# A decoder layer whose instruction order comes from a list scheduler: VectorE and GpSimd booked as taking turns, a new stage order, and a gated branch that keeps its keys as logarithms

## The chip, the core and the metric

The kernel runs on one core of a Trainium2 chip. A core has TensorE (PE, matrix products), VectorE (DVE), ScalarE (ACT), GpSimd (POOL), SyncE (SP, which starts the transfers here) and 16 DMA engines. The metric is the time of one execution on the device in microseconds. The kernel before took 1223.98 us, the median of three runs of 1223.35, 1223.98 and 1227.55 us.

## The reference, cut to what matters

One decoder layer with three token mixers side by side, for a prompt of 512 tokens and for 8 sequences of 8 new tokens (576 columns in all), everything in fp32. The model width is 1024; each mixer has 4 heads.

```python
proj = jnp.einsum('bld,dn->bln', h, w_in[l])      # aq af ai ag | bq bk bv bo bi bf | cx cg cb ca | mg
a_logf = jnp.log(lb + (1.0 - lb) * jax.nn.sigmoid(af32))
a_k = (1.0 - lb) * jax.nn.sigmoid(-af32)
# branch a (HGRN2), per chunk:
b = jnp.cumsum(fc, axis=2)
att = einsum('bhtk,bhsk,bhtsk->bhts', qc, kc, exp(b_t - b_s))     # t >= s
o = einsum('bhtk,bhkv->bhtv', qc * jnp.exp(b), S) + einsum('bhts,bhsv->bhtv', att, vc)
S_new = exp(bl) * S + einsum('bhsk,bhsv->bhkv', kc * jnp.exp(bl - b), vc)
# branch b (mLSTM): the same shape with a running maximum m and a normaliser n
# branch c (gated DeltaNet): short convolution, l2-normalised q and k, and per chunk
sol = triangular_solve(eye + a, rhs)              # a strictly lower triangular
# after the branches
z = einsum('blnc,ncd->blnd', ys, w_branch);  merged = sum(sigmoid(mg) * z)
h = layer_norm(ALPHA * h + merged @ w_out)        # LN1
gate, up = split(h @ w_ffn_in)
h = layer_norm(ALPHA * h + (silu(gate) * up) @ w_ffn_out)         # LN2
```

## The kernel before, in words

Columns of 128 features stand on the partitions and the 576 tokens (in two halves of 288) are the moving columns of a matrix product. Each fp32 product is made of three products of rounded halves, `xh*wh + xl*wh + xh*wl`. So each block of weights that lands by DMA (`wr`) is rounded by ScalarE into `wh`, and VectorE subtracts to get `wl`. A projection of 128 features, tile `p`, is 48 TensorE instructions (8 blocks of the inner dimension x 3 products x 2 halves). It can't finish before its `wl` is there.

The stages have two-letter names. `v00` to `v32` are the convolutions of branch c (first digit the head, second q, k or v), `rc` and `rb` the rows of scalar gates, `di` the inverse of the triangular matrices of branch c, `p0`-`p4` its preparations by chunk, `c1`-`c4` its chunk steps, `C0`-`C3` its sampled states. `h0`-`h3` are the heads of branch a, `a1`-`a4` and `A0`-`A3` its chunk steps and sampled states, `B1`-`B4` the chunk steps of branch b. `cA`, `aA`, `bA` load sampled states. `Z`, `X` and `Y` with a digit are the merge of the branches (gate projections, branch projections, sums), then come LN1, the feed-forward network (tiles `pq`, `us`, `fg`, `fl`, and `g` for its second product) and LN2.

Three places matter for what follows.

**The inverse in branch c** (`di`). On 64 partitions VectorE runs a recurrence over the diagonals: each step is a product `dp<-dX,dY` and a sum `dY<-dY,dp`, and each needs the one before. The rows of weights' `wl` stand in the same queue.

**The heads of branch a** (`a_head`, from L1132). Per head: the key `ak` from the gate, the cumulated log decay `ab`, and seven levels. A level computes `z`, the decay from a block's middle: a subtraction (sites `a` and `b`), one exponential, then a multiplication of one half by the key (`c`) and of the other half by the query (`d`, `z<-z,gate`), and TensorE multiplies the halves (`pz`). Twenty-eight levels in all. A last factor `akd` gives the keys decayed to the chunk's end.

**LN1.** The mean and the mean square of LN1 are first accumulated over the feature blocks (`acc<-acc,lr` and `acc<-acc,lsq`), then rounded (`ch`, `cl`), summed over the partitions by TensorE (`os`), and turned into `rstd` and `m`; then `lr<-lr,rstd`, `lr<-lr,m`, and the halves `hh`, `hl`, which the network's products read. The network's products are made by a Strassen-like scheme whose weight sums (`S`, `S3l`, `wL`, `wl`) are formed at the same time.

**What sets the order.** No instruction is issued where it is written. The `Plan` (from L61) records every operation with the tiles that it reads and writes; `schedule()` then runs the whole program on a model of the engines: it has a cost for each operation (`cost`), latencies between engines (`LAT`), free buffers, a model of TensorE's half-speed windows, and a slowdown while VectorE and GpSimd work at once (`PORT`). Always the instruction that can start first is taken, ties by priority. The priority is the place of a stage in the string `ORDER` (between `-` and `+` a stage goes one level earlier). `FLEX` lists sites whose operation may go to either of two engines; the model picks the one that would be done first. All instructions are then issued from one line, L434, so the profile's rows are told apart by tile. The chip's engines each run their own list in order and wait for one another by semaphores.

```python
for e, fn, a, k, cost, lock in o.alts:
    t = max(o.ready, eft[e]) + cost * (PSLOW if e == "POOL" else 1.0)
    ...
    if best is None or t < best:
        best = t
```

Of the kernel before, what the change touches and what calls it, by code (L numbers as in the profile page):

```python
# [11 lines left out]
ALU = mybir.AluOpType  # L12
# [51 lines left out]
class Plan:  # L64
# [35 lines left out]
    def cost(self, eng, name, out, a, k):  # L100
# [14 lines left out]
        if eng == "ACT":  # L115
            return 95 + 0.834 * n + 93 * cols
# [32 lines left out]
    def add(self, eng, name, fn, a, k):  # L149
# [47 lines left out]
    def table(self, name, after):  # L197
# [5 lines left out]
        o.cost, o.nb, o.tiles, o.alts, o.lock, o.act = 1300.0, 0, [], None, 0, 0.0  # L203
        self.ops.append(o)
# [49 lines left out]
    def schedule(self):  # L254
# [53 lines left out]
        busy = {"DVE": (0.0, 0), "POOL": (0.0, 0)}  # L308
# [30 lines left out]
        while len(order) < len(ops):  # L339
# [37 lines left out]
            if o.eng == "PE":  # L377
# [10 lines left out]
                if cold:  # L388
                    took += act
# [6 lines left out]
            elif o.eng in busy:  # L396
                dve = o.eng == "DVE"
                till, lock = busy["POOL" if dve else "DVE"]
                if o.lock and lock and till > s_:
                    v, g = (o.lock, lock) if dve else (lock, o.lock)  # L400
                    kv = PORT[v, g]
                    kg = 0.33 if v == 1 else 0.2
                    both = min(till - s_, took / (1 - kv)) if dve else min((till - s_) / (1 - kv), took)
                    mine, his = (kv, kg) if dve else (kg, kv)
                    took += mine * both
                    eft["POOL" if dve else "DVE"] += his * both
                    busy["POOL" if dve else "DVE"] = (till + his * both, lock)
                busy[o.eng] = (s_ + took, o.lock)
# [38 lines left out]
def tile_hybrid(ctx: ExitStack, tc: tile.TileContext, t):  # L447
# [1565 lines left out]
```

## Time and profile before

| what | value |
|---|---|
| runs | 1223.35, 1223.98, 1227.55 us; median 1223.98 us |
| profiled execution | 1224.88 us; span of its instructions 1223.1 us |
| TensorE busy | 1169.0 us, 96% of the span |
| VectorE, ScalarE, GpSimd busy | 857.7, 571.9, 403.6 us |
| mean granted TensorE clock | 0.968 |
| mean DMA rate | 101 GB/s |

In the page of the profile an instruction is told as line, engine, operation, `out<-in`, shape; `xN` is a count, and what stands behind the bar is the busy time in us, the mean in ns, and the idle time of the engine just before them. A granted clock of 1.00 is full speed and 0.50 is half. The view by stretches gives, for each stretch, its length, then the busy time of PE, its weight loads, DVE, ACT and POOL with the number of instructions, then the granted clock, the DMA share and GB/s. A busy TensorE at half clock does half the work, so both the idle time and the clock have to be read.

### The profile page before, as it was taken

The page shows a single profiled execution, that of the slowest core. Times are in us where ns is not written, and L with a number is a line of the kernel's source. Part 1 is how long each engine was busy: PE and PEld are TensorE (multiplying, and loading weights), DVE is VectorE, ACT ScalarE, POOL GpSimd, SP SyncE. Part 2 cuts the span into 40 slices and gives each one's busy share as a digit, 9 for nine tenths or more (in the row PEclk, how much of TensorE's full clock was granted, in tenths as well). Part 3 has the DMA queues.
Part 4 walks back from the last instruction along what each step waited for, and adds up shares of the span by engine and source line. Part 5 has one row for each costly group of instructions (what it writes and reads, how often), then busy time and mean ns, then how long its engine had stood idle before and what let it go on. Part 6 is the DMA issues. An engine that isn't in the chain of part 4 may idle for free.

```text
span 1223.1 us, 21823 instructions
## 1 busy us (share of the span) xinstructions
PE 1169.0 (96%) x8561; PEld 1132.3 (93%) x8561; DVE 857.7 (70%) x1454; ACT 571.9 (47%) x1055; POOL 403.6 (33%) x390
## 2 busy tenths in 40 slices
PE   9999998999999999899999999959999999999996
PEld 8999987899888989899999999949999999999995
DVE  4789997599775565745644448696999989873237
ACT  6467844345443734543434453553444554432234
POOL 1177623148653553102400004642200024542223
PEclk9999999999998789999999999969999999999998
DMA  8322324311122322223222432222424342533243
GB/s 259 114 100 74 94 70 130 107 52 61 53 87 96 108 91 66 60 97 100 76 82 91 147 89 76 78 70 69 133 89 145 121 157 83 179 112 93 82 115 119
DMA packets 66910, 123.08 MB, mean 101 GB/s; under 512 B 14192, under 2 KB 28272, under 8 KB 66808
## 3 DMA queue, kind: packets, MB, share of 16 engines
q1 hardware_dynamic: 66808, 121.70, 31.3%
q8 instruction: 67, 1.10, 0.4%
q14 instruction: 35, 0.29, 0.1%
HBM read 103.37 MB, written 18.17 MB: 99 GB/s over the span
## 4 chain that ended last, share of the span: by engine, by line
PE 78%; DVE 12%; ACT 4%; issue 2%; DMA 2%; POOL 1%; SPq 0%; DVEq 0%; ACTq 0%; POOLq 0%
PE p L434 25%; PE g L434 21%; PE pq L434 17%; PE tk L434 3%; PE pz L434 2%; DVE wl L434 2%; DVE lr L434 2%; PE os L434 1%; PE spo L434 1%; PE ssu L434 1%; DVE dY L434 1%; DVE dp L434 1%; PE po L434 1%; DVE num L434 1%; DVE z L434 1%
## 5 line engine op out<-in xcount | busy, mean ns | idle before, releaser
L434 DVE TENSOR_TENSOR wl<-wr,wh 128x1024 fp32r<-128x1024 f32 (+3 forms) x172 | 187.7, 1101 | 175.5 <-PE g L434 63.8
L434 ACT CAST wh<-wr 128x1024 fp32r<-128x1024 f32 (+3 forms) x192 | 156.4, 825 | 255.2 <-PE p L434 119.1
L434 PE MATMUL p<-xh,wl 128*128 128x288 f32 x960 | 213.1, 301 | 6.5 <-DVE wl L434 6.5
L434 PE MATMUL p<-xh,wh 128*128 128x288 f32 x960 | 215.3, 302 | 3.0 <-ACT wh L434 2.1
L434 PE MATMUL p<-xl,wh 128*128 128x288 f32 x960 | 213.4, 301 | 0.0
L434 PEld LDWEIGHTS p<-xh,wl 128*128 128x128 f32 x960 | 157.4, 192 | 9.0 <-DVE wl L434 7.2
L434 PEld LDWEIGHTS p<-xh,wh 128*128 128x128 f32 x960 | 157.1, 191 | 5.5 <-ACT wh L434 2.3
L434 PEld LDWEIGHTS p<-xl,wh 128*128 128x128 f32 x960 | 156.9, 191 | 1.5 <-issue 1.1
L434 PE MATMUL g<-fh,wl 128*128 128x320 f32 (+1 forms) x352 | 82.6, 295 | 0.0
L434 PE MATMUL g<-fl,wh 128*128 128x320 f32 (+1 forms) x352 | 82.3, 295 | 0.0
L434 PE MATMUL g<-fh,wh 128*128 128x320 f32 (+1 forms) x352 | 82.3, 294 | 0.0
L434 PE MATMUL pq<-hh,wh 128*128 128x288 f32 x240 | 72.5, 302 | 8.2 <-ACT hh L434 4.1
L434 PE MATMUL pq<-hh,wl 128*128 128x288 f32 x240 | 71.7, 299 | 4.1 <-DVE wl L434 4.1
L434 PE MATMUL pq<-hl,wh 128*128 128x288 f32 x240 | 71.6, 299 | 0.6 <-DVE hl L434 0.6
L434 PE MATMUL pq<-Th,wh 128*128 128x288 f32 x240 | 70.5, 295 | 0.0
L434 PE MATMUL pq<-Tl,wh 128*128 128x288 f32 x240 | 70.5, 294 | 0.0
L434 PEld LDWEIGHTS g<-fh,wl 128*128 128x128 f32 x352 | 57.1, 188 | 0.1
L434 PEld LDWEIGHTS g<-fh,wh 128*128 128x128 f32 x352 | 57.1, 188 | 0.1
L434 PEld LDWEIGHTS g<-fl,wh 128*128 128x128 f32 x352 | 57.0, 188 | 0.0
L434 PEld LDWEIGHTS pq<-hh,wh 128*128 128x128 f32 x240 | 45.8, 191 | 9.8 <-ACT hh L434 4.5
L434 POOL TENSOR_SCALAR acc<-lr 128x288 f32<-128x288 f32 (+2 forms) x4 | 4.9, 1230 | 142.2 <-DVE lr L434 142.2
L434 PEld LDWEIGHTS pq<-hh,wl 128*128 128x128 f32 x240 | 45.9, 191 | 4.3 <-DVE wl L434 4.3
(461 smaller groups left out, 3060.9 us busy)
## 6 DMA issues: line engine op xcount, KB each, us to landing
wr<-wft SPq DMA_DIRECT2D x60, 512.0 KB, 3.5
wr<-wfi SPq DMA_DIRECT2D x20, 512.0 KB, 3.6
wq<-wfi SPq DMA_DIRECT2D x40, 256.0 KB, 3.2
wr<-wfo SPq DMA_DIRECT2D x20, 512.0 KB, 3.5
wr<-wbr SPq DMA_DIRECT2D x24, 256.0 KB, 2.6
fd<-fg SPq DMA_DIRECT2D x20, 288.0 KB, 2.3
fx<-fd SPq DMA_DIRECT2D x20, 288.0 KB, 4.0
wr<-wfo SPq DMA_DIRECT2D x10, 384.0 KB, 3.1
```

Source lines behind the costliest of these rows:

```text
L434: o.fn(*o.a, **o.k)
```

## The change

Four things change together; the matrix products are the same in number (8011 matmul instructions on TensorE before and after).

1. **Branch a.** The key is kept as a logarithm too, tile `ac`: one more `scalar_tensor_tensor` gives the log of the key (with a small tile `lbl`, a logarithm of the bound), another subtracts the cumulated decay `ab`. A level's factor is then one addition to the middle value and one exponential: the 28 multiplications `c` (9 on VectorE and 19 on GpSimd) are gone, and so is the one by `akd`, 3 on GpSimd and 1 on VectorE. Eight `ac` instructions of 128x576 are new, two per head.
2. **The planner's model.** `PORT` is replaced by `held`: while one of VectorE and GpSimd holds the shared access, an instruction of the other that needs it is booked as waiting until it ends. GpSimd's costs are lower, a GpSimd choice counts double (`PSLOW` 2), results read on the same engine get a latency (VectorE 121 ns, ScalarE 131, GpSimd 40), and a TensorE instruction in a slow window is multiplied by 1.82 or 1.92.
3. **`FLEX`.** With the new list the `me` minimum of the merge (24) goes to GpSimd (23 were on VectorE), and the 24 sums of LN1 and all of the feed-forward weights' sums are on VectorE (24 and 8 were on GpSimd).
4. **`ORDER`.** The q and k convolutions come before the v convolutions, the projections of branch b's queries move behind branch b's values, and the sampled states of branch c are spread through the heads.

```diff
-ORDER = "- v20 v02 v10 + rc rb v31 v21 v32 v30 v11 v01 v00 v22 v12 p1 p2 um p3 p4 cA p0 qe cg di m2 m1 c1 m4 c2 m3 bo cs - c3 c4 C0 aA + h0 h1 h2 C1 C3 h3 a1 a2 bq a3 C2 a4 as A0 co bA A3 A2 ag A1 bv X4 ao br B1 B2 B3 ...
+ORDER = "cA - v01 rc v31 v10 rb v21 v00 v30 um v11 v20 v02 v32 v22 v12 p0 + p3 p1 aA p2 p4 qe di cg cs m1 bo c1 - + m2 C0 m3 bA c2 m4 c3 c4 h2 C1 C3 h1 h3 h0 C2 as ov a1 A0 a2 a3 A3 a4 A2 ag br A1 bv co bq ao X6 Z5 Z6 B1 B2 ...
-FLEX = "ADEFGacdhioqzIJWMNO"
+FLEX = "DWNOszjmrKuhgoJfGEbMc"
-PSLOW = 1.0
+PSLOW = 2.0
-       ("POOL", "PE"): 95.0, ("PE", "POOL"): 260.0}
-PORT = {(1, 3): 0.55, (1, 4): 0.15, (2, 3): 0.8, (2, 4): 0.35}
+       ("POOL", "PE"): 95.0, ("PE", "POOL"): 260.0, ("PE", "PE"): 0.0, ("DVE", "DVE"): 121.0,
+       ("ACT", "ACT"): 131.0, ("POOL", "POOL"): 40.0}
...
                 if cold:
-                    took += act
+                    took *= 1.92 if o.act < 0 else 1.82
...
-            elif o.eng in busy:
...
+            elif o.lock:
+                other, lag = ("POOL", 99.0) if o.eng == "DVE" else ("DVE", 43.0)
+                took += max(0.0, held[other] - lag - s_)
+                held[o.eng] = s_ + took
+                if o.fn.__name__ == "tensor_scalar" and o.eng == "POOL":
+                    held[o.eng] -= max(0.0, 0.71 * o.cost - 105.0)
...
+        c_ = sl(name="ac")
+        V.tensor_scalar(out=h2(c_), in0=ps, scalar1=-40.0, scalar2=None, op0=ALU.max)
         e = tm(name="ae")
-        V.tensor_scalar(out=h2(e), in0=ps, scalar1=-40.0, scalar2=None, op0=ALU.max)
-        S.activation(out=e, in_=e, func=AF.Exp, scale=-1.0)
+        S.activation(out=e, in_=c_, func=AF.Exp, scale=-1.0)
         sg = tm(name="asg")
         S.activation(out=sg, in_=e, func=AF.Ln, bias=one_c, scale=1.0)
+        V.scalar_tensor_tensor(out=c_, in0=c_, scalar=-1.0, in1=sg, op0=ALU.mult, op1=ALU.subtract)
...
         V.tensor_tensor_scan(b_, rst, sg, 0.0, ALU.mult, ALU.add)
+        V.scalar_tensor_tensor(out=c_, in0=c_, scalar=lbl[:, h:h + 1], in1=b_, op0=ALU.add, op1=ALU.subtract)
...
-            plan.tt("a", G if l % 2 else V, z4[:, :, 0, :], mid, b4[:, :, 0, :], ALU.subtract)
+            plan.tt("a", G if l % 2 else V, z4[:, :, 0, :], c4[:, :, 0, :], mid, ALU.add)
             plan.tt("b", V, z4[:, :, 1, :], b4[:, :, 1, :], mid, ALU.subtract)
             S.activation(out=z[:, r0:NT], in_=z[:, r0:NT], func=AF.Exp)
-            plan.tt("c", V, z4[:, :, 0, :], z4[:, :, 0, :], k4[:, :, 0, :], ALU.mult)
             plan.tt("d", G, z4[:, :, 1, :], z4[:, :, 1, :], q4[:, :, 1, :], ALU.mult)
...
-        S.activation(out=d_, in_=d_, func=AF.Exp)
-        plan.tt("D", G, k_, d_, k_, ALU.mult)
+        S.activation(out=c_, in_=c_, func=AF.Exp)
```

What this does to the queues is shown at three places. First VectorE, in the diagonal recurrence of branch c (`dp`, `dY`; `ebs`, `ge` and `gate` are small pieces of the branch, `wl` a weight block's low half). Before, ten rows from the first of four such `wl` on:

```order
L434 TENSOR_TENSOR wl_549<-wr_547,wh_548 128x1024
L434 TENSOR_TENSOR ebs_183<-sks_581,ebs_183 128x64
L434 TENSOR_TENSOR ebs_183<-ebs_183,cvs_182 128x64
L434 TENSOR_TENSOR dp_460<-dX_450,dY_451 64x207
L434 TENSOR_TENSOR dY_451<-dY_451,dp_460 64x23x9
L434 TENSOR_TENSOR dp_461<-dX_450,dY_451 64x220
L434 TENSOR_TENSOR dY_451<-dY_451,dp_461 64x22x10
L434 TENSOR_TENSOR dp_462<-dX_450,dY_451 64x231
L434 TENSOR_TENSOR dY_451<-dY_451,dp_462 64x21x11
L434 TENSOR_TENSOR dp_463<-dX_450,dY_451 64x240
```

After the change, twelve rows from the second `wl` of the recurrence on:

```order
L434 TENSOR_TENSOR wl_492<-wr_490,wh_491 128x1024
L434 TENSOR_TENSOR dY_428<-dY_428,dp_434 64x26x6
L434 TENSOR_TENSOR dp_435<-dX_427,dY_428 64x175
L434 TENSOR_TENSOR wl_510<-wr_508,wh_509 128x1024
L434 TENSOR_TENSOR dY_428<-dY_428,dp_435 64x25x7
L434 TENSOR_TENSOR dp_436<-dX_427,dY_428 64x192
L434 TENSOR_SCALAR ge_488<-ge_488 128x576
L434 TENSOR_TENSOR dY_428<-dY_428,dp_436 64x24x8
L434 TENSOR_TENSOR dp_437<-dX_427,dY_428 64x207
L434 TENSOR_TENSOR dY_428<-dY_428,dp_437 64x23x9
L434 TENSOR_TENSOR dp_438<-dX_427,dY_428 64x220
L434 SCALAR_TENSOR_TENSOR gate_489<-gate_489,par,gx_487 128x576
```

Before, behind the four `wl` in this place stand 18 rows of the recurrence (and the two of `ebs`), 19, and 25 before the fourth; after, the two `wl` shown stand three rows apart, and the next ones come behind 11, 10, 12 and 16 rows of it, with a few rows of `ge` and `gate` among them. What TensorE has to do meanwhile is more: it has 344 matmul instructions of tile `p` between the last preparation and the first product of the inverse, where it had 237.

Second TensorE, at the sampled states of branch a (`spo` and `ssu` are their outputs and updates, `po`, `su` and `tp` belong to the prompt's chunk steps, `os` is a sum for a norm). Before:

```order
L434 MATMUL spo_878<-gate_749,ss_876 128x8 x4
L434 MATMUL spo_878<-gate_749,ss_877 128x8 x3
L434 MATMUL ssu_835<-vm_834,kh_828 128x512
L434 MATMUL ssu_835<-vm_834,kl_829 128x512
L434 MATMUL os_844<-sql_842,ones_r 128x288
L434 MATMUL spo_878<-gate_749,ss_877 128x8
L434 MATMUL spo_887<-gate_685,ss_885 128x8 x4
L434 MATMUL ssu_838<-vm_837,kh_828 128x512
```

After:

```order
L434 MATMUL spo_801<-gate_755,ss_799 128x8 x4
L434 MATMUL spo_801<-gate_755,ss_800 128x8 x4
L434 MATMUL ssu_803<-vm_802,kh_791 128x512
L434 MATMUL ssu_803<-vm_802,kl_792 128x512
L434 MATMUL tp_808<-cb,ac_744 128x128
L434 MATMUL tp_808<-cb,ac_672 128x128
L434 MATMUL tp_808<-cb,ac_608 128x128
L434 MATMUL tp_808<-cb,ac_708 128x128
L434 MATMUL ssu_806<-vm_805,kh_791 128x512
L434 MATMUL ssu_806<-vm_805,kl_792 128x512
L434 MATMUL spo_834<-gate_619,ss_832 128x8
L434 MATMUL po_812<-gate_755,Sa_797 128x128
```

The sampled products that came together behind the chunk steps of branch a now lie between them.

Third LN1. Before, the last sums of the second half of the columns stood on GpSimd, in front of weight sums of the feed-forward network:

```order
L434 TENSOR_TENSOR acc_1267_1376<-acc_1267_1376,lr_1458 128x288
L434 TENSOR_TENSOR acc_1267_1376<-acc_1267_1376,lr_1467 128x288
L434 TENSOR_TENSOR acc_1268_1377<-acc_1268_1377,lsq_1494 128x288
L434 TENSOR_TENSOR acc_1268_1377<-acc_1268_1377,lsq_1496 128x288
L434 TENSOR_TENSOR acc_1267_1376<-acc_1267_1376,lr_1476 128x288
L434 TENSOR_TENSOR acc_1268_1377<-acc_1268_1377,lsq_1498 128x288
L434 TENSOR_TENSOR S_1479_1588<-wq_1582,wq_1584 128x512
```

After, they stand on VectorE, between its other work:

```order
L434 TENSOR_TENSOR acc_1267_1377<-acc_1267_1377,lr_1477 128x288
L434 TENSOR_TENSOR hl_1397<-lr_1486,hh_1389 128x288
L434 TENSOR_TENSOR S_1456_1566<-wr_1562,wr_1563 128x512
L434 TENSOR_TENSOR acc_1268_1378<-acc_1268_1378,lsq_1495 128x288
L434 TENSOR_TENSOR wr_1563<-wr_1563 128x512
L434 TENSOR_TENSOR S3l_1570<-S_1456_1566,S3h_1569 128x512
L434 TENSOR_TENSOR wr_1562<-wr_1563,wr_1562 128x512
L434 TENSOR_TENSOR wL_1572<-wr_1563,wh_1571 128x512
```

The sums now queue with the weights' rows on VectorE, and `cl<-acc,ch` comes 25 rows behind the first row shown; GpSimd keeps only the first copies of LN1's sums.

More of the change, by code (lines that the diff above doesn't have):

```diff
@@ L52 @@
     __slots__ = ("eng", "fn", "a", "k", "cost", "lat", "nb", "preds", "succs", "prio", "seq",
-                 "tiles", "start", "done", "npred", "ready", "alts", "lock", "act")
+                 "tiles", "start", "done", "npred", "ready", "alts", "lock", "act", "raw")
 def _meet(a, b):
@@ L115, in cost @@
         if eng == "ACT":
-            return 95 + 0.834 * n + 93 * cols
+            return (70 if isinstance(k.get("bias"), bass.AP) else 95) + 0.834 * n + 93 * cols
         if eng == "DVE":
@@ L126, in cost @@
             if name == "memset":
-                return 66 + 0.79 * n
+                return 60 + 0.72 * n
+            if name == "tensor_copy":
+                return 148 + 0.8 * n if n < 100 else 120 + 3.36 * n
+            if name == "tensor_scalar":
+                return 120 + 2.6 * n
             if any(0 in [st for st, _ in v.ap[1:]] for v in ap_args):
-                return 110 + 1.94 * n
-            return (740 if name == "tensor_copy" and n < 100 else 132) + {"tensor_copy": 3.7, "tensor_scalar": 2.86}.get(
-                name, 2.38) * n
+                return 126 + 1.76 * n
+            return 146 + 2.16 * n
         return 450.0
@@ L162, in add @@
             preds.update(q for q, w in self.wr.get(t, ()) if _meet(r, w))
+        o.raw = set(preds)
         for t, r in writes:
@@ L203, in table @@
         o.cost, o.nb, o.tiles, o.alts, o.lock, o.act = 1300.0, 0, [], None, 0, 0.0
+        o.raw = set()
         self.ops.append(o)
@@ L307, in schedule @@
         end = {}
-        busy = {"DVE": (0.0, 0), "POOL": (0.0, 0)}
+        held = {"DVE": 0.0, "POOL": 0.0}
         cold, wend, wact, wide = True, 1100.0, 0.0, False
@@ L395, in schedule @@
                     wend += WINDOW
-            elif o.eng in busy:
[L397 to L408, printed above, removed]
+            elif o.lock:
[4 more added lines that the diff above has]
+                    held[o.eng] -= max(0.0, 0.71 * o.cost - 105.0)
             eft[o.eng] = s_ + took
@@ L422, in schedule @@
                 u.npred -= 1
-                d = 250.0 if o.eng == "SP" else 0.0 if o.eng == u.eng else LAT.get((o.eng, u.eng), 150.0)
+                d = LAT.get((o.eng, u.eng), 250.0 if o.eng == "SP" else 150.0)
+                if o.eng == u.eng != "SP" and o.seq not in u.raw:
+                    d = 0.0
                 u.ready = max(u.ready, o.done + d)
@@ L1127, in tile_hybrid @@
     V.tensor_scalar(out=lbt[:, 3], in0=lbt[:, 2], scalar1=-1.0, scalar2=1.0, op0=ALU.mult, op1=ALU.add)
+    lbl = const.tile([P, 4], F32, name="lbl")
+    S.activation(out=lbl, in_=lbt[:, 3], func=AF.Ln)
     eblA = const.tile([P, 4, 12], F32, name="eblA")
-    akd, aqe, aatt = [], [], []
+    akd, aqe, aatt = [None] * H, [None] * H, [None] * H
     aatt_s = sl([4, 64], name="aatts")
@@ L1146, in a_head @@
         V.tensor_tensor_scan(b_, rst, sg, 0.0, ALU.mult, ALU.add)
+        V.scalar_tensor_tensor(out=c_, in0=c_, scalar=lbl[:, h:h + 1], in1=b_, op0=ALU.add, op1=ALU.subtract)
         q_, = silu_gate(IX["aq"] + h, None, 1)
         at = sl([4, P], name="aatt")
-        aatt.append(at)
+        aatt[h] = at
         def pairs(lhs, rhs, put, half=False):
@@ L1174, in vw @@
                 return ap[:, r0:NT].rearrange("p (n g i) -> p n g i", g=2, i=hh)
-            b4, k4, q4 = vw(b_), vw(k_), vw(q_)
+            b4, c4, q4 = vw(b_), vw(c_), vw(q_)
             z = sl(name="z")
@@ L1190, in a_head @@
                 pairs_s(z, z, lambda pz: V.copy_predicated(aatt_s[:64, h, :], um[:64, l, :64], pz))
-        d_ = tm(name="akd")
-        plan.tt("F", V, sview(d_), sview(b_)[:, :, 7:8].to_broadcast([P, 8, 8]), sview(b_),
-                ALU.subtract)
-        plan.tt("F", V, pview(d_), pview(b_)[:, :, 127:128].to_broadcast([P, 4, P]), pview(b_),
-                ALU.subtract)
-        S.activation(out=d_, in_=d_, func=AF.Exp)
-        plan.tt("D", G, k_, d_, k_, ALU.mult)
+        plan.tt("F", V, sview(c_), sview(c_), sview(b_)[:, :, 7:8].to_broadcast([P, 8, 8]), ALU.add)
+        plan.tt("F", V, pview(c_), pview(c_), pview(b_)[:, :, 127:128].to_broadcast([P, 4, P]), ALU.add)
+        S.activation(out=c_, in_=c_, func=AF.Exp)
         S.activation(out=b_, in_=b_, func=AF.Exp)
@@ L1201, in a_head @@
         plan.tt("D", G, q_, b_, q_, ALU.mult)
-        akd.append(k_)
-        aqe.append(q_)
+        akd[h] = c_
+        aqe[h] = q_
     Sa = {}
```

2 lines of the change are left out of this document (1 added, 1 removed).

## The prediction, made before the changed kernel was run

> **What bounds the kernel now.** I read the page first: the busy times, the clock and the chain of waits.
>
> ```profile
> span 1223.1 us, 21823 instructions
> PE 1169.0 (96%) x8561; PEld 1132.3 (93%) x8561; DVE 857.7 (70%) x1454; ACT 571.9 (47%) x1055; POOL 403.6 (33%) x390
> PEclk9999999999998789999999999969999999999998
> PE 78%; DVE 12%; ACT 4%; issue 2%; DMA 2%; POOL 1%; SPq 0%; DVEq 0%; ACTq 0%; POOLq 0%
> ```
>
> TensorE is the bound, with 96% of the span and 78% of the chain. The change leaves its products alone, so it can win only the rest: the time in which TensorE idles, and the time in which it works at half clock. I therefore went through the view by stretches, cut at the stages (columns: length; busy PE, weight loads, DVE, ACT, POOL with counts; granted clock; DMA share; GB/s).
>
> ```profile
> 43.00:46.40 3.40, 3.40 (x16) 3.40 (x15) 3.40 (x11) 1.27 (x10) 0.00 (x0) 0.51 0.74 230
> 161.00:204.00 43.00, 36.04 (x247) 34.87 (x245) 39.31 (x99) 15.82 (x23) 14.63 (x9) 0.92 0.25 67
> 240.00:384.00 144.00, 141.38 (x1073) 132.69 (x1072) 116.47 (x197) 64.49 (x113) 79.23 (x78) 0.99 0.20 65
> 388.00:412.00 24.00, 24.00 (x99) 20.43 (x99) 10.91 (x16) 12.82 (x26) 10.67 (x8) 0.57 0.33 121
> 484.00:600.00 116.00, 109.53 (x813) 106.58 (x812) 74.99 (x146) 51.50 (x124) 27.86 (x36) 0.99 0.25 79
> 600.00:770.00 170.00, 170.00 (x1286) 169.94 (x1285) 83.73 (x121) 71.92 (x108) 19.04 (x19) 1.00 0.29 94
> 770.00:845.00 75.00, 59.38 (x365) 54.97 (x364) 58.38 (x88) 39.77 (x79) 37.29 (x35) 0.84 0.22 74
> 845.00:1065.00 220.00, 216.96 (x1631) 215.52 (x1630) 204.03 (x346) 104.30 (x183) 44.54 (x28) 1.00 0.38 124
> ```
>
> The merge (600 to 770) shows the full rate: 1286 products in 170.00 us, 0.132 us each, so a projection of 48 takes 6.3 us. In the other rows length less PE is idle time, and length times (1 less clock) is about the work lost to the half clock: 7.0 and 3.4 us in the inverse (161 to 204), 2.6 and 1.4 in branch a's heads, none and 10.3 at the sampled states (388 to 412), 6.5 and 1.2 in branch b's steps, 15.6 and 12.0 at LN1, 3.0 and none in the network.
>
> **The change part by part.**
>
> *The inverse.* Four weight splits stand in VectorE's queue among the recurrence's rows. Here are their starts, the recurrence's durations (minimum, median, maximum in ns) and who waits on TensorE.
>
> ```profile
> 174.90 1.21 DVE L434 TENSOR_TENSOR wl<-wr,wh 128x1024 fp32r<-128x1024 f32 x1
> 184.31 1.21 DVE L434 TENSOR_TENSOR wl<-wr,wh 128x1024 fp32r<-128x1024 f32 x1
> 194.30 1.21 DVE L434 TENSOR_TENSOR wl<-wr,wh 128x1024 fp32r<-128x1024 f32 x1
> 203.21 1.23 DVE L434 TENSOR_TENSOR wl<-wr,wh 128x1024 fp32r<-128x1024 f32 x1 [0.50 <-PE p L434]
> L434 DVE TENSOR_TENSOR dp<-dX,dY x38: 153/328/1150, 166.8 to 201.4; 64x31 f32<-64x31 f32 x2, 64x60 f32<-64x60 f32 x2, 64x87 f32<-64x87 f32 x2, 64x112 f32<-64x112 f32 x2
> PE p L434 <- DVE wl L434: 6.5, 3, 3.5
> ```
>
> A split every 8.9 to 10.0 us feeds a TensorE that eats one in 6.3 us. The second gap, of 9.99 us with 19 recurrence rows gives (9.99 - 1.21)/19 = 0.46 us a row. After, 10 to 16 rows stand between splits, 12 in the mean: 12 x 0.46 + 1.21 = 6.7 us, and two splits stand almost together at the start, a lead of one projection. TensorE has 344 products for this place, 344 x 0.132 = 45 us, about the 43 us in which it got through 237; the other 107 come from stretches that were full. So nearly all of 7.0 + 3.4 goes; I take 9 us, between 5 (the `ge` and `gate` rows put between the splits, 0.5 and 1.0 us, delay them) and 11.
>
> *The start of branch b's gates.*
>
> ```profile
> 42.54 0.53 PE L434 MATMUL p<-xh,wh 128*128 128x288 f32 x2 [2.07 <-ACT wh L434]
> ```
>
> TensorE waits 2.07 us for a `wh` that stands behind a chain of scalar rows, and then runs one window at 0.51 (first row of the stretches), 1.7 us lost. The splits now come some rows earlier: 1.5 us, between 0 and 3.5.
>
> *Branch a's heads.* The first five rows price what goes; the next two are the nearest instructions to the new `ac` ones, of the same kind and shape; the last is TensorE's one long wait here.
>
> ```profile
> L434 POOL TENSOR_TENSOR z<-z,ak 128x256 f32<-128x256 f32 x11 | 8.7, 792 | 13.3 <-PE pz L434 7.6 <-ACT z L434 5.7
> L434 POOL TENSOR_TENSOR z<-z,ak 128x288 f32<-128x288 f32 x8 | 8.6, 1070 | 7.7 <-ACT z L434 7.6
> L434 DVE TENSOR_TENSOR z<-z,ak 128x288 f32<-128x288 f32 x4 | 4.0, 1002 | 0.3 <-ACT z L434 0.3
> L434 DVE TENSOR_TENSOR z<-z,ak 128x256 f32<-128x256 f32 x5 | 3.7, 742 | 1.3 <-ACT z L434 1.3
> L434 POOL TENSOR_TENSOR ak<-akd,ak 128x576 f32<-128x576 f32 x3 | 5.2, 1745 | 0.0
> L434 DVE SCALAR_TENSOR_TENSOR ak<-ae,lbt,asg 128x576 f32<-128x576 f32 x4 | 3.7, 930 | 0.9 <-ACT asg L434 0.9
> L434 DVE SCALAR_TENSOR_TENSOR cqkv<-cqkv,rn 128x576 f32<-128x576 f32 x4 | 3.0, 758 | 0.3 <-ACT rn L434 0.3
> PE pz L434 <- DVE aatts L434: 1.8, 1, 1.8
> ```
>
> GpSimd loses 8.7 + 8.6 + 5.2 = 22.5 us, VectorE 4.0 + 3.7 = 7.7 us and gains eight at 0.76 to 0.93, 6.1 to 7.4 us. That is much work, but TensorE is idle here for 2.6 us and slow for 1.4: what it can give is 4 us. I take 2. Against it, two of the new instructions stand in series at each head's start, and the four query projections of branch b, some 12 us of TensorE's filling by the heads' products priced at 0.132 us, are gone to later. The lower bound is -4 as a plain shortfall; the larger case is a rival.
>
> *The sampled states.* TensorE is never idle from 388 to 412 and yet at 0.57. Its work there is `spo`, with 8 moving columns; the first row gives minimum, median and maximum of its duration in ns.
>
> ```profile
> L434 PE MATMUL spo<-gate,ss x64: 215/361/362, 388.4 to 437.4; 128*128 128x8 f32 x64
> 420.00:450.00 30.00, 29.39 (x190) 26.60 (x189) 19.78 (x25) 17.05 (x28) 14.74 (x20) 0.89 0.38 117
> ```
>
> Sparse columns count little as work, so the clock falls. All 64 stay, but with dense rows of `tp`, `su` and `po` between them. At most 10.3 us here, and 0.11 x 30 = 3.3 us in the second row's stretch, can go. I take 6, between 2 (the chunk steps' own chains leave too few dense rows) and 13.
>
> The Trainium skill, "TensorE: Matmul & The Clock Gate", section "What's actually happening", ties the half clock to a whole idle window of about 3.4 us and full speed to a busy one. By that rule this stretch, busy throughout, would not be slow, and gaps of 2 us would cost no slow window: the sum below would lose its 6 us, the 3.4 of the inverse and 1 of the gates, and stand near 12. The rows 388 to 412 (24.00 busy at 0.57) and 43 to 46.4 (0.51 behind a gap of 2.07 us) disagree with it, and I go by them.
>
> *Branch b's steps.* Most of the 6.5 us is this (in total, times, longest):
>
> ```profile
> PE bnt L434 <- DVE num L434: 4.7, 4, 2.1
> ```
>  The order leaves the same kind of chain, with branch b's query projections put in front of one. 0, between -4 and 3.
>
> *The merge's minimum* goes to GpSimd.
>
> ```profile
> L434 DVE TENSOR_SCALAR me<-me 128x576 f32<-128x576 f32 x23 | 10.6, 459 | 13.0 <-ACT me L434 13.0
> L434 POOL TENSOR_SCALAR ge<-ge 128x576 f32<-128x576 f32 x7 | 12.7, 1815 | 37.1 <-ACT ge L434 27.4 <-DVE Tm L434 9.5
> ```
>
> Each takes 1.36 us longer, under the next projection's 6.3 us: nothing. Were that cover gone (at the last of them), 1.4 us.
>
> *LN1.* TensorE waits mostly for these:
>
> ```profile
> PE pq L434 <- ACT hh L434: 4.1, 1, 4.1
> PE pq L434 <- DVE wl L434: 4.1, 1, 4.1
> L434 POOL TENSOR_TENSOR acc<-acc,lr 128x288 f32<-128x288 f32 x12 | 10.9, 904 | 7.5 <-DVE lr L434 7.3
> 785.65 0.45 DVE L434 TENSOR_TENSOR lr<-g,lr 128x288 f32<-128x288 f32 x1
> 787.71 1.91 POOL L434 TENSOR_TENSOR acc<-acc,lr 128x288 f32<-128x288 f32 x2
> 791.19 1.18 DVE L434 TENSOR_TENSOR wr<-wr 128x512 f32<-128x512 f32 x1
> 802.04 0.68 DVE L434 TENSOR_TENSOR S3l<-S,S3h 128x512 fp32r<-128x512 f32 x1
> 804.45 0.82 DVE L434 TENSOR_TENSOR cl<-acc,ch 128x288 fp32r<-128x288 f32 x2
> ```
>
> A 128x512 instruction takes 1.18 us while GpSimd sums (from 787.71 on) and 0.68 alone. After, the sums are on VectorE, at 0.45 us each instead of 0.90 (0.4 from start to start), and its others stay at 0.68. But `cl` stands 25 rows behind: six of 288 columns at 0.4 and 19 of 512 at 0.62 make 14 us from about 788, 802 to 803, little before the 804.45 of now. What is won is the weights' `wl` (row one of 4.1 us) and the faster normalisation. I take 4, between -5 (weights in front of `cl` delay everything) and 8.
>
> *The network.* VectorE is 204.03 busy of 220, TensorE idle 3.0. Eight weight sums come to VectorE and the contention of GpSimd's goes: 0, between -3 and 2.
>
> **The sum**: 9 + 1.5 + 2 + 6 + 0 + 4 + 0 = 22.5 us. The order has waits that I can't price: branch b's 6.5 us and the network's 3.0 are such gaps, of 2.1 us at most, and new ones come with a new order. I take 5.5, some half of their 9.5, back. 1224.88 (the profiled execution) - 17 = 1207.9; it lies 0.9 above the median of the runs, so the forecast for the median is **1207 us**. The terms' half widths, 3, 1.7, 4.5, 5.5, 3.5, 6.5 and 2.5, taken as independent give 11: 1196 to 1218 for this case.
>
> **The rivals.**
>
> *The stalls only move* (1222 us). The inverse's gaps go, but the later chunk steps of branch c, LN1 and the sampled states keep their chains, and what is won in front is waited for there. For it: at LN1 the chain from the sums to `hh` is as long, and 27 us hang on it. Against it: the inverse's stall is a queue's rate and no chain's length. Price: 9 + 1.5 less 8 in new gaps, 2 to 3 us faster.
>
> *The half clock stays* (1215 us). `spo` keeps its 64 sparse products, and if the dense rows between wait for `Sa` and `kdt`, the windows stay slow; the 6 us, the 1.7 of the gates' window and 1 or 2 of the inverse's fall out: 17 - 9 = 8 us faster. This is also what the skill's rule gives, by another way.
>
> *Slower: the heads become the bound* (1229 us). With four projections (12 us) fewer to fill, TensorE runs into each level's chain, subtraction, exponential, GpSimd's multiplication, `pz`. If it idles 12 us in six gaps of 2 us, each brings a slow window of 1.7 us as at 43 to 46.4: 22 us, which with the 20.5 won elsewhere is level; with the 5.5 taken back as above it ends 1224.9 - 20.5 + 22 + 5.5 = 1232, and 1229 with some of these shared. It decides from about 16 us of idle time in the heads. For it: VectorE and GpSimd were 116 and 79 us busy in 144. Against it: 22.5 us of just this work goes.
>
> **How the numbers follow.** Chances: forecast 0.62, the stalls move 0.13, the half clock stays 0.10, slower 0.15. A measurement here tells 0.5% (6 us) from no change. Faster by more than that: the forecast's 0.62 and 0.08 of the half clock's, 0.70; within it 0.13 + 0.02 = 0.15; slower 0.15. The range runs from 1193 (all of the forecast's upper ends but a few) to 1224, which takes in the case that the stalls move and leaves the slower one out.
>
> **What would show it.** In the stretch of the inverse: `p <- DVE wl` near 1 us instead of 6.5 and a clock of 1.00. At the sampled states: no stretch of 24 us under 0.8. In the heads: TensorE's idle time under 6 us. At LN1: `pq <- DVE wl` under 1 us, `cl` by 803 us less what was won before, 128x512 at 0.68. I am wrong if the inverse's wait is still over 4 us, if the heads idle over 16 us, or if LN1's 75 us become longer.

## The result, and the profile after

The changed kernel took 1190.03 us (median of four runs, 1185.94 to 1192.28), the kernel before 1225.14 us on the same chip (four runs, 1223.35 to 1227.55). The ratio is 0.9708, with a 95% interval of 0.9676 to 0.9741: 35 us faster, twice the 17 that were forecast, and 3 us below the range. The profiled execution is the fastest of the four: its span is 1184.1 us against 1223.1, so 39.0 us have to be found in it.

The page of the changed kernel, its busy times, clock and chain:

```profile
span 1184.1 us, 21705 instructions
PE 1148.3 (97%) x8561; PEld 1118.5 (94%) x8561; DVE 848.3 (72%) x1506; ACT 568.7 (48%) x1052; POOL 313.9 (27%) x318
PEclk9999999999988999999999999979999999999998
PE 80%; DVE 11%; ACT 3%; POOL 3%; issue 2%; DMA 1%; SPq 0%; DVEq 0%; ACTq 0%; POOLq 0%
```

The profile counts 8561 matmul instructions on TensorE in both kernels (the 8011 given with the change is no count of this profile). TensorE's idle time (span less busy) fell from 54.1 to 35.8 us, 18.3; the other 20.7 us are busy time of TensorE. Most of that is the clock: at a mean of 0.968 before and 0.982 after, the work lost to it is 1223.1 x 0.032 = 39.1 us before and 1184.1 x 0.018 = 21.3 us after, 17.8 less.

The view by stretches, cut at the stages (the second row and the last three are for particular points below):

```profile
0.00:46.00 46.00, 43.91 (x310) 41.62 (x311) 33.20 (x89) 25.40 (x60) 4.70 (x28) 1.00 0.72 228
120.00:150.00 30.00, 26.38 (x219) 25.53 (x218) 28.87 (x68) 18.33 (x33) 13.40 (x10) 1.00 0.36 99
141.70:197.00 55.30, 51.41 (x393) 50.73 (x391) 44.93 (x116) 29.48 (x41) 3.52 (x3) 1.00 0.42 115
249.30:352.20 102.90, 102.20 (x731) 94.40 (x732) 83.00 (x141) 46.54 (x76) 50.70 (x58) 0.95 0.20 63
354.00:391.00 37.00, 37.00 (x243) 32.39 (x243) 23.83 (x39) 16.86 (x45) 13.20 (x21) 0.91 0.45 139
391.00:421.00 30.00, 30.00 (x232) 28.98 (x232) 14.82 (x27) 11.41 (x24) 8.88 (x6) 0.94 0.22 71
487.00:582.00 95.00, 92.02 (x695) 90.03 (x694) 48.52 (x102) 36.62 (x87) 28.78 (x37) 1.00 0.27 83
744.00:803.00 59.00, 49.00 (x320) 46.21 (x320) 52.50 (x101) 36.54 (x75) 15.78 (x14) 0.88 0.23 77
803.00:1029.00 226.00, 225.84 (x1702) 224.99 (x1702) 207.57 (x360) 106.67 (x187) 34.24 (x22) 1.00 0.38 124
308.00:332.00 24.00, 24.00 (x158) 23.02 (x156) 18.27 (x31) 10.11 (x17) 10.44 (x15) 0.79 0.21 65
322.00:352.00 30.00, 30.00 (x198) 28.47 (x197) 17.69 (x34) 10.62 (x17) 16.06 (x17) 0.83 0.14 45
750.00:801.20 51.20, 41.20 (x265) 38.75 (x264) 47.95 (x92) 33.52 (x69) 15.78 (x14) 0.87 0.26 88
```

The same two sums as in the prediction, idle time and length times (1 less clock), give the account. The first stretch of before, for comparison, is this:

```profile
0.00:46.00 46.00, 41.21 (x270) 39.05 (x271) 28.93 (x76) 27.09 (x71) 4.61 (x29) 0.97 0.69 224
```

| stage | lost before, us | lost after, us | gain | forecast |
|---|---|---|---|---|
| first 46 us | 4.8 + 1.4 | 2.1 | 4.1 | 1.5 |
| inverse | 7.0 + 3.4 | 3.9 | 6.5 | 9 |
| just ahead of it (120 to 141 after) | 0.3 | 3.6 | -3.3 | none |
| heads of branch a and sampled states | 4.0 + 14.2 | 5.8 + 5.1 | 7.3 | 2 + 6 |
| steps of branch b | 7.7 | 3.0 | 4.7 | 0 |
| LN1 | 27.6 | 17.1 | 10.5 | 4 |
| network | 3.0 | 0.2 | 2.8 | 0 |
| sum | | | 32.6 | 22.5, less 5.5 |

6.4 us of the 39.0 are in none of these rows. Some 3 of them are idle time and half clock outside the rows, since over the whole span the two fell by 18.3 + 17.8 = 36.1; the other 3 are in neither, and I didn't find their place.

The waits on TensorE in the changed kernel (in total, times, longest) show what is late now:

```profile
PE os L434 <- ACT ch L434: 4.2, 2, 3.5
PE pq L434 <- DVE wl L434: 3.9, 1, 3.9
PE pp L434 <- DMA Tm<-td: 3.1, 1, 3.1
PE bnt L434 <- DVE num L434: 3.0, 5, 0.7
PE qk L434 <- DVE nAT L434: 2.3, 1, 2.3
PE tp L434 <- DVE cqkv L434: 1.3, 1, 1.3
PE p L434 <- DVE wl L434: 0.8, 1, 0.8
```

`p <- DVE wl` has gone from 6.5 to 0.8 us. In its place the first product behind the inverse (`pp`) waits 3.1 us for the inverse to come back through memory, and two preparations ahead of it (`qk`, `tp`) wait 2.3 and 1.3 us for VectorE.

### The profile page after: what moved, and what is told of

Its sections match the earlier page's. It is cut to its first block, busy times and chain, and to the rows that moved or that the text cites. A ratio compares the mean times of both kernels' runs of the same rounds, so it can differ in the third digit from the quotient of the medians.

```text
span 1184.1 us, 21705 instructions
## 1 busy us (share of the span) xinstructions
PE 1148.3 (97%) x8561; PEld 1118.5 (94%) x8561; DVE 848.3 (72%) x1506; ACT 568.7 (48%) x1052; POOL 313.9 (27%) x318
## 3 DMA queue, kind: packets, MB, share of 16 engines
q1 hardware_dynamic: 66808, 121.70, 32.6%
## 4 chain that ended last, share of the span: by engine, by line
PE 80%; DVE 11%; ACT 3%; POOL 3%; issue 2%; DMA 1%; SPq 0%; DVEq 0%; ACTq 0%; POOLq 0%
PE p L434 25%; PE g L434 21%; PE pq L434 18%; PE tk L434 3%; PE pz L434 2%; DVE lr L434 2%; DVE wl L434 2%; PE po L434 1%; PE os L434 1%; DVE acc L434 1%; PE ssu L434 1%; PE spo L434 1%; POOL ce L434 1%; DVE num L434 1%; PE su L434 1%
## 5 line engine op out<-in xcount | busy, mean ns | idle before, releaser
L434 DVE TENSOR_TENSOR wl<-wr,wh 128x1024 fp32r<-128x1024 f32 (+3 forms) x172 | 183.9, 1077 | 192.9 <-PE g L434 100.7
L434 PE MATMUL p<-xh,wh 128*128 128x288 f32 x960 | 211.0, 298 | 0.4 <-ACT wh L434 0.3
L434 PE MATMUL p<-xh,wl 128*128 128x288 f32 x960 | 210.1, 298 | 0.8 <-DVE wl L434 0.8
L434 PEld LDWEIGHTS p<-xh,wl 128*128 128x128 f32 x960 | 154.9, 189 | 2.2 <-DVE wl L434 1.2
L434 POOL TENSOR_SCALAR me<-me 128x576 f32<-128x576 f32 x24 | 40.2, 1676 | 177.3 <-ACT me L434 169.4
L434 ACT CAST wh<-wq 128x512 fp32r<-128x512 f32 x60 | 34.5, 618 | 27.1 <-PE pq L434 22.7
```

The lines of the kernel that those rows point to most:

```text
L434: o.fn(*o.a, **o.k)
```

## The experiments

Every time is the median of runs on one chip, set against the kernel before on the same chip by its ratio. The runs were made on three chips, so kernels are compared with the changed kernel by their ratios (0.9708 for the changed kernel; 0.01 is 12 us); the intervals leave about 5 us either way.

### One part alone, and all but one part

The change falls into branch a's arithmetic (head), the stage order (order), the planner's model with `PSLOW` (model) and the `FLEX` list (flex). Each was put alone into the kernel before, and each was taken alone out of the changed kernel. The order is planned anew every time. The edits are the pieces of the diff shown above; for example, for order and flex alone:

```diff
-ORDER = "- v20 v02 v10 + rc rb v31 ..."
+ORDER = "cA - v01 rc v31 v10 rb v21 ..."
```

```diff
-FLEX = "ADEFGacdhioqzIJWMNO"
+FLEX = "DWNOszjmrKuhgoJfGEbMc"
```

In the two kernels with the old branch a under the new order the heads come as h2, h1, h3, h0, and the old code collects its tiles in that order: the outputs mix the heads up, while the instructions and their shapes are the same.

> The kernel before with the new branch a alone (logarithmic keys), old planner model, old FLEX, old ORDER; the order is planned anew with these. Theory A (the gain comes from where the instructions stand, and branch a's arithmetic is hidden behind TensorE): within 5 us of the kernel before, the stretch of the heads not more than 4 us shorter. Theory B (the work taken off GpSimd and VectorE is what was gained): 10 to 20 us faster.

> The kernel before with the new stage order alone. Theory A: much of the gain, 10 to 25 us faster, with the half clock at the sampled states largely gone and the inverse's wait for weights smaller; LN1 as before. Theory B: within 6 us. Theory C (the parts only work together, since the order was made for the new model): within 6 us or slower.

> The kernel before with the new planner model alone (turn taking of VectorE and GpSimd, new costs and latencies, GpSimd counted double), old FLEX, ORDER and branch a. Theory A: some gain, 5 to 12 us, at LN1 and the network, since the old model books too little for work at once. Theory C: within 6 us, since an order written for the old model is no good one for the new.

> The kernel before with the new FLEX list alone. The sums of LN1 and of the weights go to VectorE where the old model likes it. Theory A: 2 to 8 us faster, at LN1 above all. Theory C: no gain, as the old model sends other sites to GpSimd.

> The changed kernel with the old branch a (subtraction, exponential, then the multiplication by the key), all else new. Theory A: within 6 us of the changed kernel (1190), with the stretch of the heads 0 to 6 us longer. Theory B: 10 to 20 us slower than the changed kernel.

> The changed kernel with the old stage order. Theory A: 10 to 25 us slower than 1190, the sampled states at half clock again. Theory C: more than 25 us slower, the old order not made for the new model.

> The changed kernel with the old planner model (costs, latencies, slowdown by PORT, GpSimd counted once). Theory A: 5 to 12 us slower than 1190, at LN1 and the network. Theory C: as much as without the order or more, 15 us or more slower.

> The changed kernel with the old FLEX list: LN1's sums and eight weight sums may go to GpSimd again, and the minimum of the merge to VectorE. Theory A: 2 to 8 us slower than 1190, at LN1 above all. Theory C: more than 10 us slower, at places that the list doesn't touch.

| part | alone in the kernel before | ratio to before (interval) | taken out of the changed kernel | ratio to before (interval) |
|---|---|---|---|---|
| branch a | 1230.40 us | 1.0041 (1.0014 to 1.0067) | 1203.32 us | 0.9833 (0.9799 to 0.9868) |
| stage order | 1238.42 us | 1.0100 (1.0068 to 1.0133) | 1208.86 us | 0.9884 (0.9853 to 0.9916) |
| planner's model | 1222.76 us | 0.9983 (0.9960 to 1.0007) | 1228.64 us | 1.0026 (0.9999 to 1.0053) |
| FLEX | 1223.46 us | 0.9997 (0.9969 to 1.0024) | 1196.78 us | 0.9793 (0.9747 to 0.9839) |

No part gains anything alone; two lose. Taken out of the whole, each costs, by the ratios: about 10 us for FLEX, 15 for branch a, 22 for the order, and 39 for the model, which is the whole gain. That is theory C: the parts work only together. Two of its figures were missed: it asked more than 25 us of the order, which cost what theory A said (10 to 25), and for FLEX the interval does not tell its 10 us from theory A's 2 to 8. Theory B falls in its plain form: branch a's arithmetic takes GpSimd's busy time from 403.6 to 388.0 us, and alone it made the kernel slower; but taken out it costs the 10 to 20 us that theory B named. Theory A falls with the order, which alone makes the kernel 1% slower.

Where branch a's 15 us lie is seen in the heads, from the first `pz` to the last, of the changed kernel without the new branch a:

```profile
253.30:361.40 108.10, 101.25 (x718) 92.74 (x719) 87.53 (x139) 44.83 (x71) 60.47 (x64) 0.93 0.21 64
```

TensorE loses 6.9 us idle and 7.6 to the clock there, where the changed kernel loses 0.7 + 5.1: about 9 us more.

### What in the model it is

> The changed kernel, whose planner gives no latency to a result read on the same engine (the rest of its model is new). Theory A1 (this latency is what the old model lacked in VectorE's long recurrence in the inverse: rows that it booked back to back come 0.1 us later each): the wait of p for wl in the inverse comes back, 5 to 12 us slower than 1190. Theory A2 (the turn taking of VectorE and GpSimd is what matters): within 4 us.

```diff
-                if o.eng == u.eng != "SP" and o.seq not in u.raw:
+                if o.eng == u.eng != "SP":
                     d = 0.0
```

> The changed kernel with the old slowdown by PORT in place of turn taking; GpSimd's new, lower costs stay. Theory A1: within 6 us of 1190. Theory A2: 15 us or more slower, at LN1, the heads and the network, where both engines work at once.

```diff
-            elif o.lock:
-                other, lag = ("POOL", 99.0) if o.eng == "DVE" else ("DVE", 43.0)
-                took += max(0.0, held[other] - lag - s_)
+            elif o.eng in busy:
+                kv = PORT[v, g]
...
```

> The changed kernel with the old, higher costs of GpSimd and the new turn taking. Booked too long, GpSimd's work holds VectorE too long in the plan. Theory A2: 3 to 10 us slower. Theory A1: within 4 us.

```diff
-            return 146 + 2.16 * n
+            return (740 if name == "tensor_copy" and n < 100 else 132) + {"tensor_copy": 3.7, "tensor_scalar": 2.86}.get(
+                name, 2.38) * n
```

> The changed kernel with GpSimd counted once instead of double when a site chooses its engine. Theory A2: more sites go to GpSimd, where they take VectorE's turns: 5 to 12 us slower. Theory A1: within 4 us.

```diff
-PSLOW = 2.0
+PSLOW = 1.0
```

> The changed kernel with the old planner model (PORT, GpSimd's old costs, GpSimd counted once, the old rule for slow windows), to which only the latency of a result read on the same engine is added. Theory H (this latency is what the order needs): 1195 to 1208 us, most of the way from the 1228.6 of the kernel with the old model whole to 1190. Theory I (the parts of the model are needed together, and the order was made for them): 1215 us or more.

```diff
 # the changed kernel with the old model, and
+       ("POOL", "PE"): 95.0, ("PE", "POOL"): 260.0, ("PE", "PE"): 0.0, ("DVE", "DVE"): 121.0,
+       ("ACT", "ACT"): 131.0, ("POOL", "POOL"): 40.0}
...
+                d = LAT.get((o.eng, u.eng), 250.0 if o.eng == "SP" else 150.0)
+                if o.eng == u.eng != "SP" and o.seq not in u.raw:
+                    d = 0.0
```

| kernel | time | ratio to before (interval) |
|---|---|---|
| no same-engine latency | 1220.72 us | 0.9974 (0.9950 to 0.9999) |
| old PORT for turn taking | 1205.67 us | 0.9844 (0.9771 to 0.9917) |
| GpSimd's old costs | 1206.81 us | 0.9855 (0.9809 to 0.9901) |
| GpSimd counted once | 1202.96 us | 0.9849 (0.9798 to 0.9900) |
| old model, same-engine latency only | 1206.52 us | 0.9824 (0.9784 to 0.9864) |

The latency of a result that the same engine reads is the heaviest single line: without it some 32 of the 35 us are gone, and alone it brings the old model from a ratio of 1.0026 to 0.9824, 25 us (theory H). Theory A1 is right in this, but not in putting the loss at 5 to 12 us; and the turn taking, GpSimd's costs and its double count are worth 17 to 18 us each when taken out, more than either theory gave the last two. A1 and A2 are both too narrow: the four are worth more taken out one by one than they bring together.

Where the latency bites is seen in the inverse. These are starts of weight splits among the recurrence's rows, of the changed kernel:

```profile
159.44 1.21 DVE L434 TENSOR_TENSOR wl<-wr,wh 128x1024 fp32r<-128x1024 f32 x1
165.97 1.21 DVE L434 TENSOR_TENSOR wl<-wr,wh 128x1024 fp32r<-128x1024 f32 x1
172.35 1.21 DVE L434 TENSOR_TENSOR wl<-wr,wh 128x1024 fp32r<-128x1024 f32 x1
178.75 1.21 DVE L434 TENSOR_TENSOR wl<-wr,wh 128x1024 fp32r<-128x1024 f32 x1
```

and of the kernel without that latency:

```profile
155.50 1.20 DVE L434 TENSOR_TENSOR wl<-wr,wh 128x1024 fp32r<-128x1024 f32 x1
164.03 1.21 DVE L434 TENSOR_TENSOR wl<-wr,wh 128x1024 fp32r<-128x1024 f32 x1
172.54 1.21 DVE L434 TENSOR_TENSOR wl<-wr,wh 128x1024 fp32r<-128x1024 f32 x1
180.79 1.21 DVE L434 TENSOR_TENSOR wl<-wr,wh 128x1024 fp32r<-128x1024 f32 x1
```

With it the splits come every 6.4 to 6.5 us, TensorE's own 6.3; without it, every 8.3 to 8.5. A planner that takes the recurrence's rows for shorter than they are puts more of them between two splits: 16 to 22 here, against 10 to 12. The wait of `p` for `wl` itself, which theory A1 had named, came back only in part (2.0 us in that kernel); the larger loss is the wait behind the inverse. And the inverse is only a part of it. The waits of the kernel without the latency:

```profile
PE pq L434 <- ACT hh L434: 8.6, 1, 8.6
PE pp L434 <- DMA Tm<-td: 6.9, 1, 6.9
PE bnt L434 <- DVE num L434: 5.3, 4, 1.8
PE pq L434 <- DVE wl L434: 4.7, 1, 4.7
```

These are 8.6 us at LN1 (4.1 in the kernel before), 5.3 in branch b's steps (4.7 before) and 6.9 behind the inverse (3.1 in the changed kernel). Its stretches of the inverse, branch b's steps, LN1 and the network:

```profile
141.00:205.00 64.00, 55.00 (x419) 53.69 (x418) 50.52 (x122) 31.97 (x46) 5.64 (x4) 0.95 0.42 114
487.00:597.00 110.00, 103.70 (x781) 101.15 (x780) 59.66 (x126) 42.83 (x108) 31.96 (x37) 1.00 0.25 77
753.00:829.00 76.00, 56.25 (x346) 51.87 (x345) 57.62 (x100) 39.12 (x79) 24.69 (x21) 0.84 0.23 70
829.00:1062.00 233.00, 231.03 (x1725) 229.86 (x1724) 211.84 (x364) 112.59 (x195) 41.35 (x25) 0.99 0.39 129
```

By the same two sums TensorE loses 31.9 us at LN1, where the changed kernel loses 17.1, 12.2 instead of 3.9 in the inverse, 6.3 instead of 3.0 in branch b's steps, and about 4 instead of 0.2 in the network. The profiled run is that kernel's fastest, 1212.13 us; its span is only 26.2 us longer than the changed kernel's, since some 5 us less are lost at the heads and the sampled states. So this one line carries the gain of all four places. That it is VectorE's own chains that make the rows late, and not those of ScalarE or GpSimd, whose latency went with the same line, is argued; it was traced in the inverse alone.

### Is it the part, or the new plan?

Each of these kernels is planned anew, so a loss could come from any other plan being worse than one that had been picked. Two kernels ask that.

> The changed kernel with a stage order in which v10 and Z3 stand some places elsewhere, and for which the planner books the same length within 1.4 us. Theory F (an order keeps its worth when the planner books the same): within 5 us of the changed kernel. Theory G (the order was picked on the chip among many, and any other plan loses what luck had given): 7 to 15 us slower, as the reversals of single parts were.

```diff
-ORDER = "cA - v01 rc v31 v10 rb v21 ... B1 B2 Z3 X4 Z1 B3 Z7 B4 Z0 X3 ..."
+ORDER = "cA - v01 rc v31 rb v10 v21 ... B1 B2 X4 Z1 B3 Z7 B4 Z0 Z3 X3 ..."
```

> The changed kernel with another stage order and FLEX list, which the planner books 7.1 us shorter. Theory F: 3 to 8 us faster than the changed kernel, about 1183 to 1187. Theory G: no faster, or 5 to 15 us slower.

```diff
-... - + m2 C0 m3 bA c2 m4 c3 c4 h2 C1 C3 h1 h3 h0 C2 as ov a1 A0 a2 a3 A3 a4 A2 ...
+... - c1 + m3 bA C0 m4 c4 c3 c2 C2 C1 C3 h2 h1 h3 h0 a4 as a3 ov A0 A3 A2 a2 a1 ...
```

The neighbouring order took 1190.01 us (ratio 0.9679 to 0.9754), the changed kernel's 1190.03: theory F holds there, theory G does not. A plan that is booked alike runs alike, and the 10 to 39 us of the reversals are no mere price of planning anew. That is one neighbour, so it is support and no proof.

The other kernel, which has another FLEX list too, took 1175.60 us, but it tells nothing: its order puts branch a's and c's chunk steps backwards, and a step whose predecessor hasn't been planned leaves out the products with the state that it would carry on. Its page counts them, 56 fewer:

```profile
PE 1140.2 (97%) x8505; PEld 1109.6 (95%) x8505; DVE 844.6 (72%) x1493; ACT 568.4 (48%) x1046; POOL 299.1 (25%) x316
```

It is therefore not a version that beats the changed kernel, and whether a better booked order would gain stays open.

### Two engine choices, in an unchanged order

Here the order is that of the changed kernel, and only the engine of 24 instructions is another.

> The changed kernel in its own order, where only the 24 sums of LN1 (acc) are issued on GpSimd instead of VectorE, each at its place in the order. Theory D (the sums on GpSimd stretch VectorE's instructions beside them, and the end of LN1's statistics): 4 to 8 us slower than the changed kernel, in the stretch of LN1 alone. Theory E (their place is of no weight, the new order is what gains there): within 2 us.

```diff
             for o in self.schedule():
+                if o.alts and (o.eng == "DVE" and "acc" in o.k["out"].tensor.name and o.k["out"].shape[-1] == 288):
+                    o.fn = [w for w in o.alts if w[0] == "POOL"][0][1]
                 o.fn(*o.a, **o.k)
```

> The changed kernel in its own order, where only the 24 minima of the merge (me) are issued on VectorE instead of GpSimd. The prediction held their place to cost nothing: within 2 us of the changed kernel, TensorE full in the merge either way. The rival (1.2 us longer each on the chain from the projection to the gate) would make this kernel 2 us or more faster.

```diff
             for o in self.schedule():
+                if o.eng == "POOL" and "out" in o.k and o.k["out"].tensor.name.split("_")[0] == "me":
+                    o.fn = self.nc.vector.tensor_scalar
                 o.fn(*o.a, **o.k)
```

With LN1's sums on GpSimd: 1188.21 us (ratio 0.9650 to 0.9741), no slower than the changed kernel as far as the interval tells; theory D's 4 us lie at its end. LN1's stretch and the sums' row in that kernel:

```profile
744.00:803.00 59.00, 47.23 (x310) 44.41 (x310) 52.24 (x90) 35.87 (x74) 24.66 (x23) 0.88 0.24 76
L436 POOL TENSOR_TENSOR acc<-acc,lr 128x288 f32<-128x288 f32 x12 | 11.8, 983 | 10.8 <-DVE lr L436 10.8
```

and the same sums in the changed kernel:

```profile
L434 DVE TENSOR_TENSOR acc<-acc,lr 128x288 f32<-128x288 f32 x12 | 5.4, 449 | 0.1
```

The sums take 983 ns instead of 449, and 310 products instead of 320 fit in the stretch: 10 x 0.132 = 1.3 us. That is theory E: with the order as it is, their place is not what gained at LN1.

With the merge's minimum on VectorE: 1185.47 us (0.9647 to 0.9742). The intervals overlap almost wholly, and 2 us can't be told by them. The traces tell more: from the start of the first minimum to the end of the span it is 725.0 us here (455.6 to 1180.6) and 725.7 in the changed kernel (458.4 to 1184.1). So the prediction's "nothing" stands within about 1 us, and the rival's 2 us or more are not seen. TensorE was full in the merge in both. The two rows, changed kernel first, then this one:

```profile
L434 POOL TENSOR_SCALAR me<-me 128x576 f32<-128x576 f32 x24 | 40.2, 1676 | 177.3 <-ACT me L434 169.4 <-DVE wl L434 7.7
```

```profile
L436 DVE TENSOR_SCALAR me<-me 128x576 f32<-128x576 f32 x24 | 12.3, 511 | 12.7 <-ACT me L436 12.6
```

None of the complete versions is faster than the changed kernel by more than these measurements tell.

## Why the prediction was wrong

The sign, the bound (TensorE's idle and half-clock time) and the places were right: every stage with a forecast gain gained. The size was half of what came. Against the table above, 32.6 us came where 17 were forecast. Of the 15.6 us between, LN1 has 6.5, branch b's steps 4.7, the network 2.8, the first 46 us 2.6, and the 5.5 taken back, of which 3.3 came, 2.2; the inverse and the heads with the sampled states gave 3.2 less than forecast. The steps that failed:

**The planner's latencies had no term, and the gaps were taken for a property of any order** ("I take 5.5 back"). This step is the plainest failure. I left branch b's 6.5 us and the network's 3.0 where they were and took a further 5.5, some half of them, off the sum for new gaps. The old gaps fell to 3.0 and 0.2 instead; of new ones, 3.3 us came ahead of the inverse. The runs show that the gaps depend on what the planner books: with no same-engine latency branch b's steps lose 6.3 us again and the network about 4. I had listed the latencies as a part of the change and gave them nothing, while this one line is worth some 32 us of the finished kernel.

**Branch b's steps at 0** and **the network at 0**: 4.7 and 2.8 us, for that reason. I read from the order that the chain to `bnt` was still there, but not that five waits of at most 0.7 us would take the place of four of up to 2.1.

**LN1 at 4**: 10.5 us, the term that was off by most, and by another way than I said. My two signs failed: `pq <- DVE wl` is 3.9 us and not under 1, and `cl` comes 29.6 us behind the first half's `rstd` (779.59 less 750.00), where it came 29.3 behind (804.45 less 775.11). Of the changed kernel:

```profile
750.00 0.46 DVE L434 SCALAR_TENSOR_TENSOR rstd<-os,rstd 128x288 f32<-128x288 f32 x1 [1.45 <-PE os L434]
778.99 0.68 DVE L434 TENSOR_TENSOR S3l<-S,S3h 128x512 fp32r<-128x512 f32 x1
779.59 0.81 DVE L434 TENSOR_TENSOR cl<-acc,ch 128x288 fp32r<-128x288 f32 x2
```

and of the kernel before:

```profile
775.11 0.46 DVE L434 SCALAR_TENSOR_TENSOR rstd<-os,rstd 128x288 f32<-128x288 f32 x1 [1.46 <-ACT rstd L434]
```

LN1's stretch from that `rstd` to the last `hl` is as long as before, 51.2 us against this row of before:

```profile
775.10:826.90 51.80, 37.09 (x210) 33.50 (x209) 47.97 (x73) 33.37 (x67) 30.44 (x28) 0.78 0.26 87
```

What changed is how much is done meanwhile. TensorE does 265 products instead of 210, 55 x 0.132 = 7.3 us that are not left for later; VectorE does 92 instructions instead of 73 in the same 47.95 us, with GpSimd busy for 15.8 us instead of 30.4. That VectorE's instructions are shorter beside an idler GpSimd was my mechanism, with 0.68 us for 128x512 as forecast; but moving the sums back costs only 1.3 us, so the sums are not the source. What they hang on is the planner's latency, without which LN1 loses 31.9 us again; which rows of the plan let the 55 products in is not settled.

**The inverse at 9**: the row's cadence was nearly exact (6.7 us forecast, 6.4 to 6.5 measured; 0.8 us of waits left). 6.5 us came, and 3.3 were given back ahead of it. What I left out is what is late next: once TensorE is fed, it runs out of projections while the inverse comes back through memory, and the first product behind it waits 3.1 us. The recurrence itself, with six splits among its rows instead of three, took 37 us from its first sum to its last, where it took 35. The row of the sums, and that product:

```profile
L434 DVE TENSOR_TENSOR dY<-dY,dp x38: 144/319/419, 148.1 to 184.9; 32x7 f32<-32x7 f32 x2, 32x12 f32<-32x12 f32 x2, 32x15 f32<-32x15 f32 x2, 64x31 f32<-64x31 f32 x2
196.95 1.16 PE L434 MATMUL pp<-Tm,nAT 128*128 128x128 f32 x8 [3.10 <-DMA Tm<-td]
```

**The first 46 us at 1.5**: 4.1; I priced the one gap and missed that TensorE gets through more products from the start (310 instead of 270).

**The heads and the sampled states, 2 + 6**: 7.3, right in sum; the sampled products now start at 323 us, amid the heads, so the two can't be told apart. TensorE idles 0.7 us in the heads, so the slower rival, with its 16 us of idle time, is out; and branch a's arithmetic, which I had hidden behind TensorE, costs some 15 us when taken out of the changed kernel, about 9 of them in the heads. That this is because the heads have less filling in the new order is argued. The rival "the half clock stays" is out too: no 24 us are at 0.57. But my sign, none under 0.8, was missed by a hair, with 0.79 from 308 to 332; that row differs from one execution to the next, as the last section shows. (The rival's 1215 us should have been 1216 by its own 8 us.)

**The range** took the terms' errors for independent. They were not: taking out the one line of the latency moves LN1, the inverse, branch b's steps and the network the same way.

## What to carry to other kernels

Where a planner's order sets the program, an edit to its model is not a detail around the change: give it a term, and expect the errors of all stages to move together. A missing 0.1 us for a result read on the same engine is little per instruction and much along a chain, because it decides what is queued between the chain's rows. And parts of such a change can't be judged one by one from the kernel before: here no part alone gained, and each taken out of the whole cost 10 to 39 us.

## What the runs showed of the hardware that was not expected

How much half clock the sampled states meet differs between executions of one list. In the kernel with the merge's minimum on VectorE the first minimum starts at 455.6 us (458.4 in the changed kernel), and until then the two are the same program; yet in the same 30 us its row is this:

```profile
322.00:352.00 30.00, 30.00 (x226) 27.63 (x225) 24.35 (x41) 12.68 (x23) 16.59 (x18) 1.00 0.18 54
```

1.00 against 0.83, and 226 products against 198, 28 x 0.132 = 3.7 us, from one and the same list of products. One execution fell to the half clock there and the other did not, which may be a part of the 6 us between the runs of one kernel. The Trainium skill, "TensorE: Matmul & The Clock Gate", section "What's actually happening", says that the window is free-running and that the moment of the change varies with where in the window the work falls; two executions that differ here are in keeping with that. Its rule of a whole idle window does not fit the slower one: TensorE was busy for all 30.00 us in both.

A one-input instruction of 128x576 takes 1676 ns on GpSimd and 511 on VectorE, 3.3 times as long, and costs this kernel nothing that shows, under a projection of 6.3 us.
